# The constant for the gap between two matmuls, while a Tile program is scheduled

## The chip, the cores and the metric

The kernel runs on one core of one Trainium2 chip. The metric is the device time of one execution in microseconds (us); the time before is the median of three runs. Engines are named as the profile names them: PE is TensorE (PEld its weight loads), DVE is VectorE, ACT is ScalarE, POOL is GpSimd, and SP is SyncE, which issues most of the DMAs.

## The reference

The reference is a trunk of two layers over 256 frames of width 1024, in float32. Each layer norms its input, projects it with one wide matrix, runs three token mixers side by side, weighs them by sigmoid gates and adds an output projection to the residual:

```
for l in range(DEPTH):                        # DEPTH = 2
    h = _rms(x, norm_g[l])
    proj = h @ w_in[l]                        # (256, 1024) @ (1024, 9304)
    (gq, gk, gv, ga, gz, bq, bk, bv, iq, ik, iw, bz,
     cq, ck, cv, cz, gate) = jnp.split(proj, SPLIT_AT, axis=-1)
    y_a = _gla(...) * silu(gz)                # gated linear attention, chunks of 64
    y_b = _dsa(...) * silu(bz)                # indexer, top 64 keys, softmax attention
    y_c = _diff(...) * silu(cz)               # differential attention
    g = sigmoid(gate)
    merged = g0 * (y_a @ w_br[l, 0]) + g1 * (y_b @ w_br[l, 1]) + g2 * (y_c @ w_br[l, 2])
    x = x + merged @ w_out[l]
```

## The kernel before, in words

The 256 frames are two tiles of 128 (t = 0 and 1). All products are made at float32 accuracy from two halves: each operand is split into a rounded part (hi) and the remainder (lo), both in the type fp32r, and `mm3` (L287) issues three matmuls, hi by hi, hi by lo and lo by hi, into one PSUM tile.

The weights come as units of 128 x 1024 numbers (512 KB), loaded by SP into four buffers `raw`. The class `Stream` splits a unit: ACT copies it to `whi` (L234) and DVE subtracts to get `wlo` (L240); there are five buffer pairs (`BUFS["wt"]`, L98). `Stream.need` asks for units 21 places ahead of their use. A unit serves 12 matmuls in a projection (two rows of weights, two tiles t, three matmuls) and 6 in a `Pair`, which makes four of the gate blocks by seven products in place of eight; some of the sums of weights that it needs are made by DMAs on POOL that add in flight (`Stream.add`, L208).

The list `ORDER` (L36) says in which order the chunks of the projections are traced. Between the matmuls, `flow.pump` gives the mixers' tasks a turn: transposes, evacuations of PSUM, softmax, the top-k rounds. A task's matmuls are held behind the last projection matmul that was traced before them (`Tensor.put`, L111), and never the other way round.

The order in which this is written down is not the order in which the engines' queues run. When the context closes, the framework's scheduler plays the program through on a model of the core, engine by engine, and at each step gives an engine the earliest traced instruction whose inputs the model holds to be ready. An instruction whose input is late in the model is passed by later ones. So the model's durations decide the order of each queue, PE, ACT, DVE, POOL and SP alike; on the chip each queue then runs in that fixed order and waits on semaphores. Only in some places an order is written by hand: the start (L477 to L543), a few places with `ws.hold`, `order` and `issue_after`, and the tasks' matmuls. One of the model's constants is `PE_FULL_CLOCK_PASS_GAP_NS`, the time that it adds between the starts of two matmuls beyond the streaming of the columns, at the full clock; its value in the framework's table is 2.5.

At the end of a layer the output projection runs in eight blocks (L1131) in the order of input half h, output half n and tile t. Whenever a block of h = 1 is done, DVE adds it to the residual (L1146). For the first layer the sum of squares of that half follows (`sumsq` on ACT, `sumsq_v` on DVE for t = 0, n = 1), and when both halves of a tile are there, `norm_in` (L345): `norm_scale` adds up on DVE (`v`, L324) and takes the power on POOL (`r`, L325), `norm_half` scales the tile (`h`, L332) and transposes it on PE (`hps`), and `evac` (L337) writes `hTh` on ACT and `hTl` on DVE. The next layer's first projection `bq` starts with tile t = 0 alone.

What the change touches is the call in `kernel` that opens the scheduling context:

Of the kernel before, what the change touches and what calls it, by code (L numbers as in the profile page):

```python
# [2 lines left out]

# [4 lines left out]

F32 = mybir.dt.float32
F32R = mybir.dt.float32r  # L10
# [1143 lines left out]
                        behind = norm_in(l + 1, t)  # L1154


def _lay_out(inputs):
    import numpy as np

    g = {k: np.asarray(v) for k, v in inputs.items()}  # L1160
    w_in, w_br, w_out = g["w_in"], g["w_br"], g["w_out"]
    f = w_in.dtype

    def unit(w):
        n, m = w.shape
        return w.reshape(2, P, m).transpose(1, 0, 2).reshape(P, 2 * m)

    units = np.empty((L * NUNIT, P, 1024), f)
    small = np.empty((L, P, KD8 * SMALL), f)
    i = 0  # L1170
    for l in range(L):
        for name in NAMES:
            n = int(name[-1]) if name[-1].isdigit() else 0
            if name[0] == "p":
                b = int(name[1])
                parts = [w_br[l, b, h * 256:h * 256 + 256, n * CH:n * CH + CH] for h in range(2)]
            elif name.startswith("out"):
                n, h0 = int(name[3]), 512 * int(name[4])
                parts = [w_out[l, h0 + h * 256:h0 + h * 256 + 256, n * CH:n * CH + CH] for h in range(2)]
            else:  # L1180
                c = COL["gate"] + CH * n if name.startswith("gate") else COL[name]
                parts = [w_in[l, h * 256:h * 256 + 256, c:c + CH] for h in range(4)]
            for p in parts:
                units[i] = unit(p)
                i += 1
        s = np.concatenate([w_in[l, :, COL["ik"]:COL["ik"] + 64], w_in[l, :, COL["ga"]:COL["ga"] + 16],
                            np.zeros((D, 16), f), w_in[l, :, COL["iw"]:COL["iw"] + 8]], axis=1)
        small[l] = s.reshape(KD8, P, SMALL).transpose(1, 0, 2).reshape(P, KD8 * SMALL)

    pack, ptmp = np.zeros((P, NPK), f), np.zeros((P, NPT), f)  # L1190

    def put(name, a):
        dst, (s, e) = (pack, PK[name]) if name in PK else (ptmp, PT[name])
        dst[:, s:e] = a

    r = np.arange(P)
    put("m0", ((r[None, :] < r[:, None]) & (r[:, None] < 64)).astype(f))
    put("m1", (r[None, :] < r[:, None]).astype(f))
    put("ind", np.stack([(r < 64), r >= 0], axis=1).astype(f))
    put("qg", g["dsa_qn_g"].T)  # L1200
    put("kg", g["dsa_kn_g"].T)
    put("dqg", np.concatenate([g["diff_qn_g"].T] * 2, axis=0))
    put("dkg", np.concatenate([g["diff_kn_g"].T] * 2, axis=0))
    put("glag", np.broadcast_to(g["gla_norm_g"].reshape(1, L * P), (P, L * P)))
    lam = np.stack([g["diff_lq1"], g["diff_lk1"], g["diff_lq2"], g["diff_lk2"]], axis=1)
    put("lam", np.broadcast_to(lam.reshape(1, L * 4 * 64), (P, L * 4 * 64)))
    eye = np.concatenate([np.eye(P, dtype=f), g["norm_g"].reshape(L * KD8, P).T], axis=1)
    wa2b = np.zeros((P, L, 256), f)
    wa2b[64:80] = g["gla_wa2"].transpose(1, 0, 2)
    wa2b[SMALL] = g["gla_ba"]  # L1210
    x = g["x"].reshape(T, D)
    return {"x0": np.concatenate([x[:P], eye], axis=1), "x1": x[P:], "units": units, "wsmall": small, "pack": pack,
            "ptmp": ptmp, "wa2b": np.ascontiguousarray(wa2b)}
# [18 lines left out]
```

## Time and profile before

| | before |
|---|---|
| median of 3 runs | 590.84 us (590.62 to 591.07) |
| span of the profiled execution | 589.0 us |
| median of the runs less that span | 1.84 us |
| PE busy, matmuls | 581.9 us (99%), 3116 |
| PE weight loads busy | 495.2 us (84%) |
| DVE busy | 494.4 us (84%) |
| ACT busy | 382.9 us (65%) |
| POOL busy | 89.7 us (15%) |
| read from HBM | 120.21 MB, 206 GB/s over the span |

The profile is of one execution. Its span goes from the first to the last instruction; the runs' times contain 1.84 us more. Busy shares are averages over stages; a matmul's record is longer than the distance to the next one, since matmuls overlap, so the distance between starts is what tells TensorE's pace. Lines such as L119 are lines of the helper that issues all matmuls; the tiles' names tell them apart.

### The profile page before, as it was taken

The page shows a single profiled execution, that of the slowest core. Times are in us where ns is not written, and L with a number is a line of the kernel's source. Part 1 is how long each engine was busy: PE and PEld are TensorE (multiplying, and loading weights), DVE is VectorE, ACT ScalarE, POOL GpSimd, SP SyncE. Part 2 cuts the span into 40 slices and gives each one's busy share as a digit, 9 for nine tenths or more (in the row PEclk, how much of TensorE's full clock was granted, in tenths as well). Part 3 has the DMA queues.
Part 4 walks back from the last instruction along what each step waited for, and adds up shares of the span by engine and source line. Part 5 has one row for each costly group of instructions (what it writes and reads, how often), then busy time and mean ns, then how long its engine had stood idle before and what let it go on. Part 6 is the DMA issues. An engine that isn't in the chain of part 4 may idle for free.

```text
span 589.0 us, 8836 instructions
## 1 busy us (share of the span) xinstructions
PE 581.9 (99%) x3116; PEld 495.2 (84%) x3116; DVE 494.4 (84%) x815; ACT 382.9 (65%) x655; POOL 89.7 (15%) x121
## 2 busy tenths in 40 slices
PE   8999999999999999999999999999999999999997
PEld 4888888998888988888878888889888889888886
DVE  6878969988999899898687796797989998889962
ACT  6759668786658478464466775776866576656530
POOL 2032212002213031000020340300211221200000
PEclk9999999999999999999999999999999999999999
DMA  8654669428999679565446446862599994974821
GB/s 334 235 197 144 209 235 270 142 104 227 289 293 220 228 225 284 175 221 197 143 145 207 151 149 208 263 205 105 184 260 279 297 242 149 284 236 132 258 75 71
DMA packets 34027, 121.82 MB, mean 207 GB/s; under 512 B 3776, under 2 KB 4160, under 8 KB 33984
## 3 DMA queue, kind: packets, MB, share of 16 engines
q1 hardware_dynamic: 29376, 104.49, 50.5%
q0 software_dynamic: 4608, 16.78, 15.9%
q8 instruction: 24, 0.39, 0.3%
q14 instruction: 19, 0.16, 0.1%
HBM read 120.21 MB, written 1.05 MB: 206 GB/s over the span
## 4 chain that ended last, share of the span: by engine, by line
PE 96%; DVE 1%; DMA 1%; ACT 1%; issue 0%; POOL 0%; SPq 0%; DVEq 0%; POOLq 0%
PE q L119 13%; PE p L119 11%; PE gate L119 7%; PE out L119 7%; PE bz L119 4%; PE iq L119 4%; PE gq L119 4%; PE ck L119 4%; PE cq L119 4%; PE gz L119 4%; PE cz L119 4%; PE gv L119 4%; PE bv L119 4%; PE bk L119 4%; PE cv L119 4%; PE bq L119 3%
## 5 line engine op out<-in xcount | busy, mean ns | idle before, releaser
L234 ACT ACTIVATE whi<-raw 128x1024 fp32r<-128x1024 f32 x172 | 180.9, 1062 | 102.2 <-PE p L119 21.0
L240 DVE TENSOR_TENSOR wlo<-raw,whi 128x1024 fp32r<-128x1024 f32 x172 | 207.9, 1219 | 38.9 <-ACT whi L234 37.6
L234 ACT ACTIVATE whi<-sum 128x1024 fp32r<-128x1024 f32 x32 | 34.1, 1065 | 24.1 <-PE gz L119 5.4
L240 DVE TENSOR_TENSOR wlo<-sum,whi 128x1024 fp32r<-128x1024 f32 x32 | 39.5, 1235 | 4.2 <-ACT whi L234 3.7
L208 POOL DMA_DIRECT2D sum<-in_units x32 | 28.3, 883 | 84.0 <-DMA sum<-in_units 28.2
L294 POOL TENSOR_SCALAR v<-ss 128x4 f32<-128x4 f32 (+1 forms) x24 | 6.9, 288 | 224.0 <-DVE ss L398 91.5
L295 POOL TENSOR_TENSOR r<-v,half 128x4 f32<-128x4 f32 (+1 forms) x24 | 35.5, 1477 | 2.0
L119 PE MATMUL out<-wlo,mTh 128*128 128x512 f32 (+1 forms) x72 | 26.2, 368 | 0.0
L119 PE MATMUL out<-whi,mTh 128*128 128x512 f32 (+1 forms) x72 | 26.0, 366 | 0.0
L119 PE MATMUL out<-whi,mTl 128*128 128x512 f32 (+1 forms) x72 | 25.7, 368 | 0.0
L119 PE MATMUL q<-whi,sl 128*128 128x512 f32 x64 | 25.2, 394 | 0.0
L119 PE MATMUL q<-wlo,sh 128*128 128x512 f32 x64 | 25.1, 392 | 0.0
L119 PE MATMUL q<-whi,sh 128*128 128x512 f32 x64 | 24.9, 390 | 0.0
L119 PE MATMUL gate<-wlo,hTh 128*128 128x512 f32 x64 | 24.9, 390 | 0.0
L119 PE MATMUL p<-wlo,yTh 128*128 128x512 f32 x64 | 24.9, 389 | 0.0
L119 PE MATMUL gate<-whi,hTl 128*128 128x512 f32 x64 | 24.8, 390 | 0.0
L119 PE MATMUL p<-whi,yTl 128*128 128x512 f32 x64 | 24.6, 389 | 0.0
L119 PE MATMUL gate<-whi,hTh 128*128 128x512 f32 x64 | 24.5, 393 | 0.0
L119 PE MATMUL p<-whi,yTh 128*128 128x512 f32 x64 | 24.1, 392 | 0.0
L119 PE MATMUL q<-whi,hTh 128*128 128x512 f32 x48 | 19.2, 400 | 0.0
L119 PE MATMUL q<-whi,hTl 128*128 128x512 f32 x48 | 18.8, 391 | 0.0
L119 PE MATMUL q<-wlo,hTh 128*128 128x512 f32 x48 | 18.8, 391 | 0.0
(352 smaller groups left out, 1748.8 us busy)
## 6 DMA issues: line engine op xcount, KB each, us to landing
raw<-in_units SPq DMA_DIRECT2D x176, 512.0 KB, 4.5
sum<-in_units POOLq DMA_DIRECT2D x32, 512.0 KB, 7.9
sum<-in_units SPq DMA_DIRECT2D x16, 512.0 KB, 6.1
wsr<-in_wsmall SPq DMA_DIRECT2D x2, 416.0 KB, 7.0
xe<-in_x SPq DMA_DIRECT2D x1, 584.0 KB, 3.4
x<-in_x SPq DMA_DIRECT2D x1, 512.0 KB, 7.9
out<-xe SPq DMA_DIRECT2D x2, 256.0 KB, 2.0
pt<-in_ptmp SPq DMA_DIRECT2D x1, 384.0 KB, 9.5
```

The costliest lines, as they stand in the source:

```text
L119: return self.put(nc.tensor.matmul(*a, **k))
L208: G.dma_start(self.sums[l, "t3" if what == "t3" else "t1", pair, i], units[u + i], accum_op=OP.add)
L234: a = A.activation(hi, raw, AF.Copy)
L240: self.splits[j] = (a, V.tensor_sub(lo, raw, hi.bitcast(F32)))
L294: G.tensor_scalar(v, ss, 1.0 / dim, EPS, op0=OP.mult, op1=OP.add)
L295: G.tensor_tensor(r, v, half[:, :n], op=OP.pow)
```

## The change

While the scheduling context is open, the constant of the framework's table is set to 13.3, and set back when the context has closed. The new context manager is entered ahead of the tile context and left after it, so the scheduling lies inside it. No instruction of the kernel is written differently.

```
+from concourse.hw_specs import get_hw_spec
...
+@contextmanager
+def matmul_gap(ns):
+
+    spec = get_hw_spec("TRN2")
+    kept, spec.PE_FULL_CLOCK_PASS_GAP_NS = spec.PE_FULL_CLOCK_PASS_GAP_NS, ns
+    try:
+        yield
+    finally:
+        spec.PE_FULL_CLOCK_PASS_GAP_NS = kept
...
-    with tile.TileContext(nc, schedule_with_timeline_sim=True) as tc:
+    with matmul_gap(13.3), tile.TileContext(nc, schedule_with_timeline_sim=True) as tc:
         trunk(tc, *args, out)
```

More of the change, by code (lines that the diff above doesn't have):

```diff
@@ L1 @@
 import math
-from contextlib import ExitStack
+from contextlib import ExitStack, contextmanager
 import concourse.bass as bass
```

## The prediction, made before the changed kernel had run

> **What bounds the kernel now.** I read the page first, then the chain of waits, then TensorE's own waits, then the busy time by stage, and at last the one place where TensorE stands still.
>
> ```profile
> span 589.0 us, 8836 instructions
> ...
> PE 581.9 (99%) x3116; PEld 495.2 (84%) x3116; DVE 494.4 (84%) x815; ACT 382.9 (65%) x655; POOL 89.7 (15%) x121
> ...
> PEclk9999999999999999999999999999999999999999
> ...
> PE 96%; DVE 1%; DMA 1%; ACT 1%; issue 0%; POOL 0%; SPq 0%; DVEq 0%; POOLq 0%
> ```
>
> TensorE is busy for 99% of the span, at the full clock in every slice, and 96% of the chain that ended last is TensorE behind itself. The span of 589.0 us stands against a median of 590.84 us for the runs, so 1.84 us lie around it; I add them unchanged. A busy matmul row is no proof that nothing is lost, so the spacing comes next. These are pieces of the chain (start, length, count):
>
> ```profile
> 198.46 6.99 PE bz L119 x58
> 207.97 0.44 PE yT L122 x4
> 209.01 10.91 PE gate L119 x48
> 456.49 10.99 PE gz L119 x48
> ```
>
> The 48 gate matmuls of 512 columns take 10.91 us, 227.3 ns each; the 58 of bz, of 256 columns, take 120.5 ns each. The 256 further columns cost 106.8 ns, so 512 columns are 213.6 ns of streaming and 13.7 ns are left per matmul. The change's 13.3 ns is that remainder as I read it, to 0.4 ns. The worst such piece of 48 that is shown (gz) is 0.08 us longer. So inside a stage TensorE runs at its own pace. What it waits for, in all the span:
>
> ```profile
> PE idle L119 <- DVE idle L463: 1.2, 1, 1.2
> PE bq L119 <- DVE wlo L492: 1.0, 2, 0.9
> PE hps L122 <- DVE h L332: 0.6, 1, 0.6
> PE hps L122 <- ACT h L332: 0.5, 1, 0.5
> PE bq L119 <- ACT hTh L341: 0.2, 1, 0.2
> ```
>
> The first three belong to the first 16 us, where lists of orders written by hand fix ACT, DVE and POOL (lines 477 to 543). The last two are the joint between the two layers. Between 16 us and the joint, and from there to the end, no TensorE wait is listed at all.
>
> **The change part by part.** It adds, removes and resizes no instruction on the chip: 3116 matmuls, 172 + 32 weight splits, the DMAs of the SP and POOL queues all stay. What it changes is the pace at which the planner lets TensorE go while it decides orders. By the framework's listing the constant stands at 2.5 ns, so the planner has priced a 512-column matmul at about 216 ns and will now price it at about 227. I count the consequences by place.
>
> *The matmul stream.* 0 us. The pace on the chip is not the planner's. A place in the queue may change, but each matmul keeps its 227 or 120 ns.
>
> The Trainium skill, TensorE: Matmul & The Clock Gate, section "Wait — 56ns, not 53.3ns?", puts the start-to-start time of warm matmuls at the streaming time plus about 2.5 ns, 215.7 ns for 512 columns. By that rule the change would give the planner a wrong pace, 11 ns too slow; the sum would not move by it, but an order made for a slower TensorE would leave it waiting (the second rival does that by other means). The 227.3 ns above do not agree with it; for this kernel's matmuls the row decides.
>
> *The interior of the stages (17 to 290 us, 310 to 585 us).* The splits that feed TensorE, and the busy time by stage:
>
> ```profile
> L234 ACT ACTIVATE whi<-raw 128x1024 fp32r<-128x1024 f32 x172 | 180.9, 1062 | 102.2 <-PE p L119 21.0
> L240 DVE TENSOR_TENSOR wlo<-raw,whi 128x1024 fp32r<-128x1024 f32 x172 | 207.9, 1219 | 38.9 <-ACT whi L234 37.6
> ...
> 17.00:150.00 133.00, 133.00 (x737) 114.42 (x736) 112.56 (x184) 98.60 (x181) 24.56 (x33) 1.00 0.61 197
> 150.00:225.00 75.00, 75.00 (x431) 65.88 (x430) 70.27 (x140) 48.21 (x87) 17.34 (x23) 1.00 0.88 248
> ...
> 438.00:513.00 75.00, 75.00 (x431) 65.89 (x430) 69.34 (x140) 48.34 (x87) 15.11 (x22) 1.00 0.88 247
> ...
> DVE wlo L240 <- ACT whi L234: 18.8, 23, 2.1
> ...
> 294.04 1.06 ACT L234 ACTIVATE whi<-raw 128x1024 fp32r<-128x1024 f32 x1 [0.30 <-PE out L119]
> ```
>
> (The window rows give TensorE, weight loads, DVE, ACT, POOL, clock, DMA share, GB/s; then DVE's wait with the largest total between 16 and 289 us: total, times, longest; then one split of the timeline with the idle time before it.) ACT stands idle 102.2 us ahead of its splits, most of it until TensorE lets go of a buffer: the weights wait for TensorE, not the reverse. The lead is worked out from the five buffer pairs: the pair that TensorE releases is split in 1.06 + 1.22 us, with 0.3 us, the idle time before such a split, for the hand-over 2.6 us (estimate), and is needed four units later. A unit is 6 matmuls in a pair product and 12 in a projection, so four are 5.4 to 10.9 us, and 2.8 to 8.3 us remain. Any change of order on ACT, DVE, POOL or SP that makes a split late by less than 2.8 us is hidden by TensorE's own queue. Cost taken: 0. Bounds: no gain, since no wait is there to remove; a loss only beyond the lead (second rival).
>
> *Moved DMAs.* Raw loads on SP and accumulating loads on POOL may start earlier or later, since each waits for a split or a DVE result ahead of it. Nothing is added to either queue, and whoever waits for a load is a split, with the lead above. 0, by the same cover; if the cover is gone it is the second rival's price.
>
> *The joint of the layers.* Here the cover is missing, because every matmul of the next layer needs the norm of this one's sum. In order of time, from the timeline:
>
> ```profile
> 289.00 0.69 DVE L1146 TENSOR_TENSOR xe<-out,xe 128x512 f32<-128x512 f32 x1 [0.85 <-PE out L119]
> 292.40 0.69 DVE L1146 TENSOR_TENSOR xe<-out,xe 128x512 f32<-128x512 f32 x1 [2.71 <-PE out L119]
> 293.13 0.69 DVE L314 CUSTOM_DVE_ANT_0 junk<-xe 128x512 f32<-128x512 f32 x1
> 293.75 0.08 DVE L314 DVE_READ_ACCUMULATOR2_ANT ss<- 128x1 f32 x1
> 293.99 0.69 DVE L1146 TENSOR_TENSOR x<-out,x 128x512 f32<-128x512 f32 x1 [0.16 <-PE out L119]
> 294.60 0.15 DVE L324 SCALAR_TENSOR_TENSOR v<-ss 128x1 f32<-128x1 f32 x1
> 294.90 1.42 POOL L325 TENSOR_TENSOR r<-v,half 128x1 f32<-128x1 f32 x1 [70.00 <-DVE v L324]
> 296.28 0.39 PE L119 MATMUL out<-whi,mTl 128*128 128x512 f32 x1
> 296.36 1.34 ACT L332 ACTIVATE h<-xe,r 128x512 f32<-128x512 f32 x2 [1.25 <-POOL r L325]
> 297.13 1.27 PE L122 MATMUL hps<-xe,h 128*128 128x128 f32 x8 [0.46 <-ACT h L332]
> 298.61 0.50 PE L119 MATMUL bq<-whi,hTh 128*128 128x512 f32 x1 [0.21 <-ACT hTh L341]
> ```
>
> After the last matmul of the layer starts (296.28) TensorE could go on at 296.51; the next layer's first starts at 298.61. Of these 2.10 us the eight transposes need 0.88 (twice the 0.44 of four), so 1.22 us are lost, and that is all that an order can win here. Two orders made by the planner stand in this chain. First, the t = 0 half is complete at 292.40, 3.40 us after its sibling, which is 15 matmuls for a tile that has 12: matmuls of a later tile were put ahead, because the planner held a weight to be late. Each such matmul taken out brings the chain 0.227 us forward. Second, DVE adds x (293.99) before it makes v (294.60), though v's input was there at 293.83: the add stood first, since by the planner its matmuls were done first. In the planner's count these are 7 matmuls (1.59 us on the chip); at 216 ns they were 1.51 us, now they are 1.59, so the add becomes ready 0.08 us later and v may go first. That would be worth 294.60 − 293.83 = 0.77 us in the chain, and on TensorE at most what it waits there. Bounds: −1.22 us when both turn the right way, and +0.227 us for each further matmul put ahead, up to the 7 of the next tile that are still behind, +1.6 us. I take −0.2 us, one matmul fewer ahead and the add still before v: the add's input came 0.16 us after v's on the chip and yet was put first, and the correction supplies half of that.
>
> *The tail.* The last add and store follow the last matmul directly; their order comes from data. 0.
>
> Sum on the profiled execution: 589.0 + 0 + 0 − 0.2 + 0 = 588.8; with 1.84 around it 590.6 us.
>
> **The rivals.**
>
> *The joint closes.* Matmuls of the later tile are no longer put ahead and v goes before the add: the chain is 0.68 + 0.77 = 1.45 us earlier, and TensorE's 1.22 us there go. For it: both orders come from a pace that the rows show to be wrong by 5%. Against: the evacuation between transposes and first projection (0.21 us of listed wait) hangs on ACT and DVE, not on the planner's pace, and half the effect may stay. 590.84 − 1.22 = 589.6 us; with a wait of the t = 1 half 589.4.
>
> *DVE becomes the bound between gz and bz.* In the 75 us from 150 and again from 438 us DVE works 70.27 and 69.34 us, so only 4.7 and 5.7 us of it are free. DVE works its queue in order. If the new order puts evacuations or top-k rounds ahead of a split whose input is not there, each costs as much as DVE's longest such wait, 2.1 us. It decides from 4.7 + 2.8 = 7.5 us of added waits in a layer (free time, then the lead), or four such waits: 8.4 − 7.5 = 0.9 us of TensorE idle in the first layer, about as much in the second: 590.84 + 1.8 = 592.6 us. For it: 94% of DVE. Against: a slower TensorE in the plan brings the plan's DVE into more slack, not less, so fewer things should be squeezed.
>
> *The setting changes nothing.* The planner may have taken its copy of the constant, or its decisions may not turn on 11 ns. Then the queue orders are equal and the time is 590.84. Against: an order by readiness turns on such differences (0.08 us above).
>
> The Trainium skill, Perfetto Trace Analysis, section "Identifying the Most-Contended Engine", would judge TensorE's room by the weight loads' share, here 84%, and not by the 99%. By that 16% of the span would be open to a better order; no run here shows so much room, since the spacing is even and no wait is listed.
>
> **How the numbers follow.** What a measurement of this kernel can tell from no change is about 0.2%, 1.18 us. The forecast, small shifts at the joint: 0.50, 590.6 us, its own range 589.9 to 591.4. The joint closes: 0.20, 589.4 to 589.7, mostly just beyond the bound. DVE becomes the bound, or the joint takes up to 1.6 us more: 0.20, 592.0 to 592.6. Nothing changes: 0.10. Faster takes nearly all of the second case, 0.18; slower the third but a little, 0.18; within the bound the first and the fourth and what is left, 0.64. The range reaches down to the closed joint and up to the price of the second rival without its worst part: 589.3 to 592.3.
>
> **What would show it.** The same count of matmuls and the same 227 ns in the gate pieces; TensorE's waits still only in the first 16 us and at the joint; there, the spacing of the adds (3.40 and 1.59 us now) and the places of v and of the x add. A TensorE wait on a split anywhere between 17 and 290 us would say that the lead is smaller than I work out; more than 1.3 us gained would say that TensorE lost time that I did not see; equal queues would say that the setting did not arrive.

## The result and the profile after

The changed kernel takes 594.65 us (median; 593.27 to 596.05) against 590.88 us (590.62 to 591.07) of the kernel before: a ratio of 1.0064, 95% interval 1.0047 to 1.0082. It is slower, by 3.8 us, and outside the forecast range.

The page of the changed kernel, from an execution of 596.05 us, the longest of its four:

```profile
span 594.3 us, 8843 instructions
...
PE 585.3 (98%) x3116; PEld 495.4 (83%) x3116; DVE 497.7 (84%) x815; ACT 382.5 (64%) x655; POOL 84.9 (14%) x121
...
PE 77%; DVE 12%; issue 4%; DMA 4%; ACT 1%; POOL 0%; SPq 0%; DVEq 0%; ACTq 0%; POOLq 0%
```

The work is the same, 3116 matmuls. But TensorE's share of the chain that ended last fell from 96% to 77%, and VectorE (12%) and weight loads by DMA (4%) took its place. Where TensorE waits (total, times, longest):

```profile
PE bz L120 <- DVE wlo L241: 1.3, 2, 0.6
...
PE bz L120 <- ACT whi L235: 0.7, 2, 0.4
PE go L120 <- DVE Sl L303: 0.7, 1, 0.7
PE go L120 <- ACT Sh L302: 0.4, 2, 0.2
PE bq L120 <- ACT hTh L342: 0.2, 1, 0.2
```

The wait for hps at the joint (0.5 us before) is gone. New are waits at `bz` and at the matmuls `go` of the gated attention, in both layers, at the place that the prediction called covered. How much each place costs is read from tiles that stand outside it. First the kernel before, then after (behind the durations stand the first and the last start; `p` with yTh begins in layer 1 after the stage, and its last start is in layer 2):

```profile
L119 PE MATMUL iq<-hTh,whi x64: 277/283/365, 111.5 to 413.8; 128*128 128x256 f32 x64
...
L119 PE MATMUL p<-whi,yTh x64: 389/389/444, 229.3 to 555.3; 128*128 128x512 f32 x64
```

```profile
L120 PE MATMUL iq<-hTh,whi x64: 277/283/365, 111.7 to 416.8; 128*128 128x256 f32 x64
...
L120 PE MATMUL p<-whi,yTh x64: 389/389/445, 233.0 to 560.7; 128*128 128x512 f32 x64
```

The delay is 0.2 us at the first `iq`, 3.7 us at the first `p`, 3.0 us at layer 2's last `iq`, and 5.4 us at its last `p`. So layer 1 loses 3.5 us between `iq` and `p`, 0.7 us comes back by the next `iq` (the joint), and layer 2 loses another 2.4 us in the same stretch. The listed waits there add up to 3.1 us only; idle time is counted from the modelled end of a matmul's row, which is later than the next start could be. An example: from the `bz` matmul at 201.30 us to the next at 202.22 it is 0.92 us, where two `bz` are 0.12 us apart elsewhere; 0.80 us are lost, and 0.64 are listed.

What happens in that stretch is best seen at 10 us a window. The kernel before (TensorE, weight loads, DVE, ACT, POOL, clock, DMA share, GB/s):

```profile
170.00:180.00 10.00, 10.00 (x46) 8.28 (x45) 9.45 (x21) 5.31 (x7) 1.98 (x3) 1.00 0.90 252
180.00:190.00 10.00, 10.00 (x64) 8.90 (x62) 10.00 (x20) 9.52 (x20) 4.34 (x4) 1.00 0.99 223
190.00:200.00 10.00, 10.00 (x73) 9.34 (x72) 8.41 (x14) 4.83 (x12) 0.00 (x0) 1.00 0.84 280
```

VectorE has 2.1 us free in these 30 us, much the same share as the 4.7 us in 75 that the prediction read. What that average hid is the middle row: from 180 to 190 us nothing is free, so a delay that begins there isn't made up before 190 us. After:

```profile
170.00:180.00 10.00, 10.00 (x46) 8.28 (x45) 9.96 (x20) 3.71 (x4) 1.73 (x2) 1.00 0.90 287
180.00:190.00 10.00, 10.00 (x60) 8.52 (x58) 10.00 (x20) 9.48 (x19) 3.09 (x3) 1.00 0.81 199
190.00:200.00 10.00, 9.10 (x59) 7.72 (x58) 10.00 (x18) 4.30 (x13) 2.44 (x3) 1.00 0.95 244
...
150.00:225.00 75.00, 73.14 (x415) 62.99 (x414) 70.42 (x139) 46.18 (x86) 16.19 (x22) 1.00 0.84 233
438.00:513.00 75.00, 73.74 (x419) 63.91 (x418) 70.58 (x140) 48.08 (x88) 14.05 (x20) 1.00 0.85 241
```

VectorE now has no free time up to 200 us but 0.04 us, and over the 75 us it works hardly longer than before (70.42 against 70.27 us). Pieces of the timeline show two changes. Before (start, length, engine, line, operation; in brackets the idle time ahead of it and its releaser):

```profile
178.27 0.60 ACT L419 ACTIVATE th<-gz 128x512 f32<-128x512 f32 x1 [0.93 <-PE gz L119]
179.00 1.06 ACT L234 ACTIVATE whi<-sum 128x1024 fp32r<-128x1024 f32 x1
179.74 1.09 POOL L1125 TENSOR_TENSOR gz<-gz,pk 128x512 f32<-128x512 f32 x1 [4.45 <-DVE gz L421]
180.44 1.48 DVE L240 TENSOR_TENSOR wlo<-sum,whi 128x1024 fp32r<-128x1024 f32 x1
181.39 0.36 ACT L688 ACTIVATE bp<-blog,negm 128x128 f32<-128x128 f32 x1
182.83 1.21 DVE L240 TENSOR_TENSOR wlo<-sum,whi 128x1024 fp32r<-128x1024 f32 x1
183.00 1.99 POOL L1125 TENSOR_TENSOR gz<-gz,pk 128x512 f32<-128x512 f32 x1
```

and after:

```profile
180.24 0.37 ACT L689 ACTIVATE bp<-blog,negm 128x128 f32<-128x128 f32 x1 [2.61 <-DVE negm L722]
182.10 1.08 ACT L235 ACTIVATE whi<-sum 128x1024 fp32r<-128x1024 f32 x1
184.06 1.08 POOL L1126 TENSOR_TENSOR gz<-gz,pk 128x512 f32<-128x512 f32 x1 [6.41 <-DVE gz L422]
184.16 2.06 DVE L241 TENSOR_TENSOR wlo<-sum,whi 128x1024 fp32r<-128x1024 f32 x1
187.15 2.58 DVE L241 TENSOR_TENSOR wlo<-sum,whi 128x1024 fp32r<-128x1024 f32 x1
187.25 1.40 POOL L1126 TENSOR_TENSOR gz<-gz,pk 128x512 f32<-128x512 f32 x1
```

First, the four exponentials of the top-k attention now stand on ScalarE ahead of the gate tanhs and the two splits of summed weights. They wait 2.61 us for VectorE's `negm`, and ScalarE's splits behind them start 3.1 us late. Second, the sum splits on VectorE meet GpSimd's gain multiplies otherwise. Before, the first split began when 0.39 us of a multiply were left, and the second began ahead of the other multiply, which was the one that took longer (1.99 us). Now both splits meet nearly a whole multiply, and take 2.06 and 2.58 us in place of 1.48 and 1.21. The chain of waits shows how that reaches TensorE (start, length, what):

```profile
193.59 1.14 DVE wlo L241
...
194.75 4.99 DMA raw<-in_units
...
199.85 1.07 ACT whi L235
...
200.94 1.24 DVE wlo L241
...
202.22 1.34 PE bz L120 x9
```

A late split on VectorE frees a raw buffer late; the load of the next weights takes 5 us, and its own split ends at 202.18 us; `bz`, which had waited 0.64 us for it, goes on at 202.22.

The joint after:

```profile
297.57 0.16 DVE L325 SCALAR_TENSOR_TENSOR v<-ss 128x1 f32<-128x1 f32 x1
...
298.82 0.68 DVE L1147 TENSOR_TENSOR x<-out,x 128x512 f32<-128x512 f32 x1
...
299.92 0.39 PE L120 MATMUL out<-whi,mTl 128*128 128x512 f32 x1
...
300.15 1.27 PE L123 MATMUL hps<-xe,h 128*128 128x128 f32 x8
301.63 0.50 PE L120 MATMUL bq<-whi,hTh 128*128 128x512 f32 x1 [0.21 <-ACT hTh L342]
```

Here `v` stands ahead of the x add. From the start of the last `out` to `bq` it is 1.71 us, where it was 2.33.

### The profile page after: what moved, and what is told of

Read it like the earlier page. It is cut to its first block, busy times and chain, and to the rows that moved or that the text cites. A ratio compares the mean times of both kernels' runs of the same rounds, so it can differ in the third digit from the quotient of the medians.

```text
span 594.3 us, 8843 instructions
## 1 busy us (share of the span) xinstructions
PE 585.3 (98%) x3116; PEld 495.4 (83%) x3116; DVE 497.7 (84%) x815; ACT 382.5 (64%) x655; POOL 84.9 (14%) x121
## 4 chain that ended last, share of the span: by engine, by line
PE 77%; DVE 12%; issue 4%; DMA 4%; ACT 1%; POOL 0%; SPq 0%; DVEq 0%; ACTq 0%; POOLq 0%
PE p L120 11%; PE gate L120 7%; PE out L120 7%; PE q L120 7%; DVE wlo L241 5%; PE iq L120 4%; PE gq L120 4%; PE cq L120 4%; PE ck L120 4%; PE cz L120 4%; PE bk L120 4%; PE cv L120 4%; PE bz L120 3%; PE bq L120 3%; DMA raw<-in_units 2%
## 5 line engine op out<-in xcount | busy, mean ns | idle before, releaser
L241 DVE TENSOR_TENSOR wlo<-sum,whi 128x1024 fp32r<-128x1024 f32 x32 | 43.4, 1358 | 6.8 <-ACT whi L235 6.7
L296 POOL TENSOR_TENSOR r<-v,half 128x4 f32<-128x4 f32 (+1 forms) x24 | 30.8, 1285 | 2.0
L120 PE MATMUL bz<-hTh,wlo 128*128 128x256 f32 x64 | 18.4, 289 | 1.3 <-DVE wlo L241 1.3
L120 PE MATMUL bz<-hTh,whi 128*128 128x256 f32 x64 | 18.5, 290 | 0.7 <-ACT whi L235 0.7
```

Source lines behind the costliest of these rows:

```text
L120: return self.put(nc.tensor.matmul(*a, **k))
L241: self.splits[j] = (a, V.tensor_sub(lo, raw, hi.bitcast(F32)))
L296: G.tensor_tensor(r, v, half[:, :n], op=OP.pow)
```

## The experiments

The theories: T1, the exponentials on ScalarE make the sum splits late; T2, the collision of VectorE's splits with GpSimd's multiply; T3, a late memset on GpSimd ahead of the first top-k round (`m` waits 2.4 us for it after, 0.4 before, in layer 1); T4, no one place, any other order loses. T5 came up on the way: the loss goes through the raw buffers. The kernel before measured 590.77 to 590.81 us beside all of these.

**Another value of the constant.** At 6, ScalarE's order in the stage is the old one, at 12 the new one.

```
-    with matmul_gap(13.3), tile.TileContext(nc, schedule_with_timeline_sim=True) as tc:
+    with matmul_gap(6), tile.TileContext(nc, schedule_with_timeline_sim=True) as tc:
```

> The kernel after with the constant at 6 instead of 13.3. ScalarE's queue between gz and bz then stands as in the kernel before (the two sum splits ahead of the four exponentials), while v stands ahead of the x add at the joint, as in the kernel after. If the late sum splits are the loss (T1), this run has the joint's gain of about 0.6 us and not the loss: 590.0 to 590.5 us, TensorE waiting nowhere on the splits of bz. If any shuffling of the orders costs time (T4, diffuse: 882 of TensorE's 3116 queue places differ from before, against 1006 in the kernel after), it lies near the kernel after: 593 to 595.

Measured: 591.02 us (590.57 to 591.44), ratio 1.0003 (0.9995 to 1.0012). No TensorE wait on a split of `bz` or at `go`; TensorE's queue nevertheless differs from the kernel before in 882 of its 3116 places. So other orders as such cost little, against T4. In the same trace VectorE waits up to 2.3 us for GpSimd's memset and nothing is lost there, so T3 by itself falls too. The joint's 0.6 us did not show in the time: `bq` of layer 2 starts 0.23 us earlier than before, and the rest went in places where no wait is listed. That part of the expectation missed.

> The kernel after with the constant at 12. The four exponentials stand ahead of both sum splits on ScalarE, as at 13.3, while the rest of the queues differs in 100 and more places from it. By T1 it is as slow as the kernel after: 593.3 to 596. If the loss comes from one unlucky order elsewhere (T3 or T4), it may come out anywhere from 590 to 595.

Measured: 592.82 us, ratio 1.0032 (1.0019 to 1.0046), with executions from 590.48 to 596.16. The new ScalarE order loses again, yet not in every execution. The same queues sometimes lose next to nothing, which would fit a lead that they just about use up. What varies from one to the next was not separated; in the longest, a lower granted clock is part of it (last section). The median is a little below what T1 gave.

**The exponentials put back.** `silus` and `exps` collect the gate tanhs and the exponentials; `ws.splits` holds the splits.

```
                 if c == "gz":
+                    for e in exps[0]:
+                        order(e, silus[-1])
+                        order(e, ws.splits[l * NPLAN + USE["A5"][1]][0])
```

> The kernel after with one thing written by hand: the four exponentials of the first top-k round of each layer are held behind the second gate tanh and the second sum split on ScalarE, as the kernel before has them. By T1 the sum splits start about 3 us earlier, TensorE's waits between 184 and 203 us and between 470 and 493 us go, and the time falls to 590.0 to 591. By T2 (the collision of DVE's sum splits with the gain multiply on GpSimd, which the earlier split order also takes apart) the same, with the sum splits back at 1.2 to 1.5 us on DVE. By T3 (GpSimd's late memset ahead of the first top-k round) it gains at most 1 us: 593.5 or more. By T4 no change from the kernel after: 594 to 595.

Measured: 590.49 us (590.22 to 591.93), ratio 0.9998 (0.9989 to 1.0006). One order on ScalarE in each layer takes the loss away. The joint's gain is in this time: `v` first on the kernel before brings 590.17 us by itself (below), so some 0.3 us of loss may be left. The multiplies still run beside the splits, but now the split starts first:

```profile
180.54 1.22 DVE L241 TENSOR_TENSOR wlo<-sum,whi 128x1024 fp32r<-128x1024 f32 x1
...
180.78 1.94 POOL L1132 TENSOR_TENSOR gz<-gz,pk 128x512 f32<-128x512 f32 x1 [4.91 <-DVE gz L424]
```

The split keeps its 1.22 us, and the multiply takes 1.94 us where it took 1.08.

**The converse, in two steps.** On the kernel before, the exponentials first, once with both sum splits directly behind them, and once with the order exponentials, tanh, split, tanh, split of the kernel after.

```
+                    for i in (*silus[-2:], ws.splits[l * NPLAN + USE["A5"][0]][0]):
+                        order(i, exps[0][-1])
```

> The converse: the kernel before (constant at 2.5) with the two gate tanhs and the first sum split held behind the four exponentials on ScalarE, in both layers. By T1 this alone makes the loss: 593 to 596, with TensorE waiting at bz for a split. By T3 and T4, which need other parts of the new order, it stays at 590.6 to 591.5.

Measured: 591.16 us (590.99 to 592.26), ratio 1.0010 (1.0001 to 1.0019). T1 alone falls: splits that start some 2 to 3 us late cost 0.35 us. They take 1.22 and 1.21 us here, as the multiplies come after them.

```
+                    s0, s1 = (ws.splits[l * NPLAN + u][0] for u in USE["A5"][:2])
+                    for a, b in ((silus[-2], exps[0][-1]), (s0, silus[-2]), (silus[-1], s0), (s1, silus[-1])):
+                        order(a, b)
```

> The kernel before with ScalarE's order of the kernel after at this place, written by hand in both layers: four exponentials, gate tanh, sum split, gate tanh, sum split. The run with the exponentials first but both sum splits ahead of both tanhs cost only 0.35 us, its DVE sum splits at 1.22 and 1.21 us. If lateness times collision is the cause (T2: the tanh between the splits lets VectorE finish one gate half, GpSimd's gain multiply starts on it, and VectorE's sum splits run beside it at 2.0 to 2.6 us instead of 1.22), this run has the long splits again and lies at 593 to 596. If the rest of the new order is needed (T4), it stays near 591.2 even with the exponentials first.

Measured: 596.92 us (596.02 to 597.78), ratio 1.0104 (1.0090 to 1.0118). A tanh between the splits turns 0.35 us into 6.1, of which some 1.7 us are a lower granted clock of TensorE (an estimate, in the last section). The second split takes 2.55 us, and ScalarE, which works in order, adds to it:

```profile
196.98 1.06 ACT L234 ACTIVATE whi<-raw 128x1024 fp32r<-128x1024 f32 x1 [5.50 <-DMA raw<-in_units]
197.94 0.61 ACT L301 ACTIVATE Sh<-sd 128x512 fp32r<-128x512 f32 x1
```

A weight split waits 5.50 us for its load, and the evacuation `Sh`, for which the `go` matmuls of TensorE wait 2.1 us in this layer and 2.0 in the next, stands behind it.

**The collision taken away, and made alone.** On the kernel after, the gain multiplies held on GpSimd behind the next accumulating load; then left out; then the first of these edits on the kernel before.

```
-                        G.tensor_tensor(g3, g3, pkc("glag", l * P, l * P + P).unsqueeze(1).to_broadcast([P, 4, P]),
+                        gain = G.tensor_tensor(g3, g3, pkc("glag", l * P, l * P + P).unsqueeze(1).to_broadcast([P, 4, P]),
                                         op=OP.mult)
+                        order(gain, ws.adds[l * NPLAN + USE["A5"][1]])
```

> The kernel after with GpSimd's two gain multiplies of each layer held behind the accumulating load of the second sum split on GpSimd's own queue; ScalarE's and TensorE's orders stay those of the kernel after, all work stays. T2: the first sum split is back at 1.22 us and the second too, since no multiply runs beside them; of the loss of 3.8 us most goes: 590.3 to 591.5. If the 3 us of lateness from the exponentials is the main part (T1), it gains only what the two splits get shorter, about 1 us: 593 to 594.

Measured: 593.55 us (592.60 to 593.83), ratio 1.0043 (1.0029 to 1.0057). The time is that of T1, but the trace says otherwise. The splits are back at 1.21 us, and the collision has moved to the next VectorE operation, which takes 2.89 us in place of 0.68:

```profile
186.76 2.48 POOL L1126 TENSOR_TENSOR gz<-gz,pk 128x512 f32<-128x512 f32 x2
...
186.91 2.89 DVE L904 TENSOR_TENSOR sd<-carry,decay 128x512 f32<-128x512 f32 x1
```

> The kernel after without the gain multiply of the GLA gate (the norm's gain is left out of the computation; two multiplies on GpSimd per layer are gone, nothing else). T2: sum splits at 1.22 us, 590.2 to 591.5. T1: 593 to 594, as the exponentials still stand first.

Measured: 590.75 us (590.38 to 592.41), ratio 1.0006 (0.9997 to 1.0015). With the multiplies gone altogether, the loss is gone, though the exponentials still stand first.

> The kernel before, its sum splits early, with GpSimd's two gain multiplies of each layer held behind the accumulating load of the second sum split, so that they run beside other VectorE work (the sd multiply, 2.89 us in place of 0.68 when this was done to the kernel after). If a collision of some 2 us is enough by itself (T2 alone), it costs as much as in the kernel after: 592.5 to 594. If it needs the 3 us of lateness from the exponentials as well (T1 and T2 together against one lead), it is hidden: 590.6 to 591.2.

Measured: 590.78 us (590.62 to 590.86), ratio 0.9999 (0.9990 to 1.0007), with the collision there:

```profile
185.39 2.43 DVE L903 TENSOR_TENSOR sd<-carry,decay 128x512 f32<-128x512 f32 x1
```

So it costs nothing by itself. Four of these runs make a square (layer 1; `sd` is the operation `sd<-carry,decay`):

| second sum split ends | `sd` takes | first `iq` to first `p` | run | time |
|---|---|---|---|---|
| 183.82 us (early) | 0.68 us | 117.8 us | exponentials put back | 590.49 us |
| 183.82 us (early) | 2.43 us | 117.7 us | multiplies late, kernel before | 590.78 us |
| 185.81 us (late) | 0.68 us | 117.9 us | multiplies left out | 590.75 us |
| 185.79 us (late) | 2.89 us | 119.0 us | multiplies late, kernel after | 593.55 us |

The first three columns are of the profiled executions. The first, third and fourth rows are the kernel after with one edit, and have the joint's gain of 0.6 us in their times. Two us late costs some 0.3 us, within the spread of its run; 2 us of collision costs nothing; both together cost 2.8 us over the two layers. T1 and T2 draw on the same lead. How long that lead is can be read from layer 1, which takes 117.8 us from the first `iq` to the first `p` in the kernel before: lateness and collision are 2.0 + 2.2 = 4.2 us, 1.2 us are lost, so about 3.0 us were hidden (estimate). In the profiled execution of the changed kernel the second split ends at 189.73 us, 5.7 us later than before (184.04), and 3.5 us are lost, so about 2.2 us were hidden.

The changed kernel is a little worse than the last row. Its exponentials start at 180.24 us in that execution and at 178.54 us in the two late runs: the first top-k round of layer 1 had waited 2.4 us for the memset, where these wait 0.7 to 0.8 us with nearly the same queues. By this T3 adds to the lateness and is not a cause of its own.

**The raw buffers.** Five in place of four, on the order that lost most; the room came from two other tiles, and the second run has only those given up.

```
-BUFS = dict(w2=8, kp=28, w4=8, ev=2, raw=4, wt=5, ahead=21)
+BUFS = dict(w2=7, kp=27, w4=8, ev=2, raw=5, wt=5, ahead=21)
```

> The kernel of the run with exponentials, tanh, split, tanh, split written by hand on ScalarE (596.9 us), with five raw buffers in place of four; to make room, one of the eight small work tiles and one of the 28 kept tiles are given up. The chain of its trace reads: VectorE's late split frees a raw buffer, the load of the next weights takes 4.8 us, then ScalarE's and VectorE's split, then TensorE. If this loop through the raw buffer is what turns lateness into TensorE idle time (T5), one more buffer gives about one unit more of lead (1.4 to 2.7 us of TensorE work) and most of the 6.1 us go: 591 to 593. If the loop plays no part, and the splits themselves are the limit, 596 to 598 as without it.

> The control for the run with five raw buffers: the same hand-written order, seven small work tiles and 27 kept tiles, but four raw buffers. By T5 it stays as slow as the order alone: 595.5 to 598. If giving up the two tiles is what changes the time, it goes with the run with five raw buffers.

Measured: 597.85 us (597.57 to 597.89) with five raw buffers, 593.40 us (593.01 to 593.85) with four. Both missed their expectations, and they don't tell T5 apart: with other buffers the planner made other orders, and the exponentials start at 182.56 us in the first and near 178.9 us in the second. Again the later run is the slower. So the queues were written down, instruction by instruction, as the kernel after has them on all four engines:

```
+    for names in json.loads(zlib.decompress(base64.b85decode(QUEUES))).values():
+        names = [f"I-{n}" for n in names if f"I-{n}" in made]
+        for a, b in zip(names, names[1:]):
+            tc.add_manual_dep(made[b], a, NOSYNC, reason="order")
```

> The kernel after with the order of each of the four engines' queues written down instruction by instruction as it stands there (TensorE, VectorE, ScalarE, GpSimd: no place differs), and five raw buffers in place of four; one of eight small work tiles and one of 28 kept tiles are given up for the room. If the way goes through the raw buffers (T5), loads start one unit earlier, ScalarE no longer waits for raw at 194 to 201 us, and at least half of the 3.8 us goes: 590.3 to 592.5. If the way goes straight through VectorE's and ScalarE's queues, 593.3 to 596 as in the kernel after.

> The control: the same written-down orders and the same two tiles given up, but four raw buffers. It should be the kernel after again, 593.3 to 596; if it isn't, the given-up tiles matter and the run with five raw buffers says nothing on T5.

Measured: 599.65 us (599.53 to 600.01) with five, 600.83 us (600.09 to 601.48) with four. The control isn't the kernel after again: the two tiles given up make `negm` 2.0 us later (181.50 against 179.47 us in the kernel after) and the time 6.2 us longer. Against this control the fifth raw buffer gains 1.2 us of the 10.0 that are lost. ScalarE's waits for raw loads, with five and then with four:

```profile
ACT whi L121 <- DMA raw<-in_units: 3.2, 4, 1.1
```

```profile
ACT whi L121 <- DMA raw<-in_units: 15.2, 15, 2.7
```

They fall by 12 us and the time by 1.2. By its own expectation the pair then says nothing on T5 in the kernel after; it does for this later kernel. With four buffers the chain of waits in layer 1 runs through a raw load (196.70 us, 5.36 us long) to `bz` at 204.54 us; with five it runs along VectorE's full queue up to the split that ends at 203.24 us, and `bz` goes on at 203.28. So at this lateness T5 falls as the main way: the fifth raw buffer is worth 1.2 us of the loss, and by these chains most of the rest comes through VectorE's queue. How the 3.8 us of the kernel after itself divide is open.

**The joint.** On the kernel before, `v` ahead of the x add; then also the square of x (t = 1, first half) behind the evacuations of t = 0.

```
+                if l + 1 < L and (t, n) == (1, 0):
+                    order(xadd, vs0[0])
...
-                    if (t, n) == (1, 1):
+                    if t == 1:
                         order(square, behind[0])
```

> The kernel before with one order written by hand at the joint: the last x add of layer 1 (t = 1, first half) behind v of t = 0 on VectorE, as the kernel after has it; nothing else. By the prediction's step on the joint v comes 0.77 us earlier, and on TensorE at most what it waits for hps, 0.6 us, goes: 590.1 to 590.3, TensorE's listed wait for hps under 0.2 us. If the joint is bound by something else: 590.8.

Measured: 590.17 us (590.09 to 590.36), ratio 0.9990 (0.9982 to 0.9999). As expected: `v` comes at 293.97 in place of 294.60 us, and `bq` at 298.03 in place of 298.61. (At the joint TensorE's listed wait for hps is 0.5 us; the 0.6 us that the expectation names belong to the first 16 us.)

> The kernel before with v ahead of the x add, and also the square of x (t = 1, first half) behind the evacuations of hps of t = 0 on ScalarE, where it now stands ahead of them and holds them 0.79 us. If ScalarE's queue is what the first projection of layer 2 still waits for, bq starts up to 0.5 us earlier: 589.6 to 589.9. If the transposes or VectorE's evacuations set it, 590.2 as with v alone.

Measured: 589.77 us (589.68 to 589.96), ratio 0.9982 (0.9973 to 0.9991), 1.0 us below the kernel before and the fastest of all. ScalarE was what `bq` still waited for:

```profile
297.23 2.02 ACT L341 ACTIVATE hTh<-hps,xe 128x128 fp32r<-128x128 f32 x7
...
297.67 0.48 PE L119 MATMUL bq<-whi,hTh 128*128 128x512 f32 x1
```

**Both repairs at the constant 13.3.** The edit with the exponentials and the one of the square.

> The kernel after (constant 13.3, v already ahead of the x add) with the four exponentials of each layer held behind the sum splits, as in the run that brought 590.49 us, and the square of x (t = 1, first half) held behind the evacuations of t = 0 as in the run that brought 589.77 us on the kernel before. If the stage and the joint are independent, 590.49 minus the 0.4 us that the square brought: 589.9 to 590.2. If the new orders still lose time elsewhere, above 590.3.

Measured: 589.95 us (589.67 to 591.80), ratio 0.9991 (0.9983 to 1.0000). With two orders written by hand the changed constant does as well as the old one with its two (589.77 us), within the spread of its runs; it brings nothing of its own.

## Why the prediction was wrong

The step that failed is "the interior of the stages", costed at 0. The prediction took it that no new order would make a split later than the lead covers, with more slack in the plan as its only reason. In the changed kernel the second sum split of layer 1 ends 5.7 us later than before; the stretch from `iq` to `p` loses 3.5 us in layer 1 and 2.4 us in layer 2 of the profiled execution.

*The lead.* Its size was about right: 2.8 us at the least by the prediction, 2.2 to 3.0 us by the rows of layer 1 above. But it was set against a single late split. The square shows that lateness and lost VectorE time add up: about 2 us of each alone is hidden, 4.2 us together are not. It was also assumed that the unit's raw data lie ready; in the chain after, the load is late as well.

*VectorE's room.* The second rival set its point at 7.5 us of added waits, 4.7 of them free VectorE time over 75 us. Here 4.2 us already cost time: in the ten us that matter VectorE has nothing free. Its direction was right (a split behind work whose input isn't there) and its price, 592.6 us, 2 us too low; it shared 0.20 of the chances with a longer joint. It looked on VectorE's queue for what the wait turned out to be on ScalarE's: four exponentials (1.38 us in all) that wait 2.61 us with ready splits behind them.

*The argument against it.* "A slower TensorE in the plan brings the plan's DVE into more slack" did not hold. The order on ScalarE turns somewhere between 6 and 12 ns; why the planner lets the exponentials pass was not looked at.

*The collision.* The prediction named no contention at all, though the trace before has it: a sum split of 1.48 us at 180.44, beside 1.21 for the other, and a multiply of 1.99 us beside one of 1.09.

*The matmul stream, moved DMAs and tail.* The pace is the same: in the chain of the kernel after, 48 gate matmuls take 10.90 us, 227.1 ns each. No loss stands in the tail. The moved loads were costed by the same cover as the splits and fell with it.

*The joint.* Here the forecast gain came by the other of its two orders. The −0.2 us that was taken stood for one matmul fewer put ahead, with the x add still before `v`. But the 15 matmuls where 12 were needed did not change (3.40 us between the adds, before and after), and `v` did go first, which brings 0.6 us alone. With one more order 1.0 of the 1.22 us could be had. The first rival, the closing joint, came half true.

*The setting changes nothing* fell: 1006 places of TensorE's queue changed.

## What to carry to other kernels

Read an engine's free time in windows as short as the lead, not over a stage: 94% busy over 75 us was 100% in the ten us that counted. Small delays on different engines that end in the same split add up against one lead, so cost them together, and look at what stands in order behind an instruction that waits. A more exact constant in a planner need not give a better order; where two or three orders matter, write them down by hand, and let the planner keep the rest.

## What was not expected of the hardware

In these kernels VectorE and GpSimd hold each other off. Beside the multiply that began at 184.06 us, the split that began 0.10 us later took 2.06 in place of 1.22 us; where the split began first, the multiply took 1.94 in place of 1.08 (both shown above). The one that comes second seems to wait for the other's end: 184.06 + 1.08 + 1.22 = 186.36, and the split ended at 186.22. The Trainium skill, SBUF — State Buffer, section "Who interferes with whom", says so: a VectorE instruction with two inputs in SBUF and a GpSimd instruction that reads SBUF meet at a port pair that the two engines share, and the one that starts first keeps the other out until it is done. These rows agree within 0.15 us; the second pair (187.15 and 187.25) does not show who came first, as GpSimd's spans are rough.

TensorE's granted clock can fall after a short stall. The run with tanh and split in turn, in layer 2, behind a wait of 2.0 us:

```profile
490.00:492.00 2.00, 2.00 (x14) 2.00 (x13) 2.00 (x4) 2.00 (x11) 0.52 (x1) 0.62 0.83 283
492.00:494.00 2.00, 2.00 (x12) 2.00 (x12) 1.00 (x4) 0.85 (x1) 1.41 (x3) 0.53 0.75 221
```

The clock is 0.62 and 0.53 for 4 us, which costs some 1.7 us (an estimate: 2 × 0.38 + 2 × 0.47); in each of the four executions of this kernel the mean granted clock is 0.997. The stall of 2.1 us in layer 1 of the same execution left it at 1.00. The Trainium skill, TensorE: Matmul & The Clock Gate, section "What's actually happening", puts the fall to half speed behind an idle window of about 3.4 us; here it came behind less. So a stall's price is not fixed, and this is one source of the spread of the kernels that stall, 590.48 to 596.16 us with the constant at 12, where the kernel before keeps within 0.6 us. In the execution of 596.16 us the clock is 0.70 and 0.50 in the two windows of 2 us from 200 us on.
